# A linear-attention kernel on one Trainium2 core: the last three output stores move from SP's hardware DMA queue to GpSimd's software DMA queue

## The chip, the core and the metric

The kernel runs on one core of one Trainium2 chip. The metric is device time in microseconds (us) of one execution. TensorE (PE), VectorE (DVE), ScalarE (ACT), GpSimd (POOL) and SyncE (SP) each run their own instruction stream; transfers between HBM and the on-chip memory SBUF are issued by SP (a queue that the profile calls hardware_dynamic) or by GpSimd (software_dynamic), and are carried by 16 DMA engines.

## What is computed

Q, K and V have shape (8, 12, 512, 64), float32. For each of the 96 heads:

```
Qf = maximum(0, Q) + 1;  Kf = maximum(0, K) + 1
KV = Kf^T V                      # 64 x 64
out = (Qf KV) / (Qf sum(Kf) + 1e-10)
```

There is no softmax and no 512 x 512 matrix. Each input is read once (12.58 MB each, 37.75 MB in all), and 12.58 MB are written.

## The kernel before

The 96 heads are 48 pairs, four pairs to a group, so there are 12 groups (NG = 12, `last` = 11). Two groups share one step's input tiles and one output tile: `outs[s]` with s = g // 2 holds the results of groups 2s and 2s + 1, and a group's own part of it is every second slot, 4 slots of 512 floats in each of 128 partitions, 1 MiB.

**Loads.** `load` (L105), `load_q` (L119) and `load_rest_q` (L96) are issued on GpSimd, since they also convert float32 to bfloat16; each input's two groups come in one DMA that puts 1 MiB into SBUF (2 MiB out of HBM). Only the first half-step of Q is loaded plain, over SP (L93). Input tiles have two buffers, so a load waits until the buffer's former content has been consumed.

**Compute.** `k_features` and `q_features` (L146, DVE) make the features; `v_blocks` (L157; L164 on DVE, L162 on ACT) puts V into a block layout whose extra columns of ones give the sum of Kf; `keys_values` (L175) multiplies on PE and ACT copies the result; `transposes` (L193) turns the query features; `out_matmuls` (L206) multiplies, and `norms` (L223; L231 reciprocal, L232 multiply, both on DVE) divides and writes the float32 result into `outs`. Each group's `norms` is four pairs of a reciprocal and a multiply.

**Stores.** `store(g)` (L131) writes group g's 1 MiB. The order of everything is written out by hand (L256 on). Stores 0 to 4 are issued in loop turn 7, store 5 in turn 8, store 6 in turn 9, store 7 after that, and stores 8 to 11 at the very end (L313), each on its engine's instruction stream behind whatever that engine was given before. Stores 0 to 9 go over GpSimd (L135). Store 10 goes over SP (L138), and store 11 goes over SP as two halves (L141): the first may leave when head half h = 0 of group 11 has been normalized, the second after h = 1.

**The end of the program.** After the last store SP waits (as L340 in the profile) in turn for the completion of every DMA and of the other engines' work. All five engines then meet at a barrier, GpSimd clears the semaphores, and they meet once more. Each engine drains itself (a DRAIN instruction, also L340) before it signs in at the barrier.

**Semaphores of the software queue.** GpSimd's DMAs use eight completion semaphores in turn. The DMA that reuses a semaphore is held until the DMA eight places before it has landed; for store g that is store g - 8 from g = 8 on, and a load before that.

Of the kernel before, what the change touches and what calls it, by code (L numbers as in the profile page):

```python
# [19 lines left out]
def kernel(  # L20
# [19 lines left out]
    nc = tc.nc  # L40
# [8 lines left out]
    NP = 4  # L49
    NG = NPAIR // NP  # L50
# [36 lines left out]
    outs = {}  # L87
# [43 lines left out]
    def store(g):  # L131
        s = g // 2
        o_to = o_dram[:, 2 * NP * s : 2 * NP * s + 2 * NP]
        if g < NG - 2:
            nc.gpsimd.dma_start(out=o_to[:, g % 2 : 2 * NP : 2], in_=outs[s][:, g % 2 : 2 * NP : 2])  # L135
            return
        if g == NG - 2:
            nc.sync.dma_start(out=o_to[:, 0 : 2 * NP : 2], in_=outs[s][:, 0 : 2 * NP : 2])  # L138
            return
        for h in range(2):  # L140
            nc.sync.dma_start(  # L141
                out=o_to[:, 2 * h + g % 2 : 2 * NP : NP], in_=outs[s][:, 2 * h + g % 2 : 2 * NP : NP]
            )

    def feature(dst, src):
        nc.vector.tensor_scalar(  # L146
# [109 lines left out]
    with tc.manual_schedule():  # L256
# [18 lines left out]
        for g in range(last - 1):  # L275
            if g % 2:
                transposes(g - 1)
            k_features(g)
            v_blocks(g)
            if g >= 2:  # L280
                output(g - 2)
            if g % 2:
                transposes(g)
            else:
                q_features(g)
                q_features(g + 1)
            keys_values(g)
            if g % 2 and g // 2 + 2 < NG // 2:
                load_pair(g // 2 + 2)
            if g == NG - 5:  # L290
                for done in range(g - LAG):
                    store(done)
            if g >= NG - 5:
                store(g - LAG)
# [5 lines left out]
        v_blocks(last)  # L300
        keys_values(last - 1)
        store(last - 1 - LAG)
        q_features(last - 1)
        q_features(last)
# [40 lines left out]
```

## Time and profile before

| | |
|---|---|
| Time, median of 3 runs | 126.48 us (126.4 to 126.58) |
| Time of the profiled execution | 126.1 us |
| Its span, from the first to the last instruction | 124.3 us |
| Mean granted TensorE clock | 0.823 |
| Busy: DVE, PE, ACT, POOL | 89.6, 63.5, 59.6, 25.7 us |
| Packets: software queue, hardware queue | 10592 and 1216 |
| Last multiply of group 11 (L232) starts | 112.85 us |
| Last store issued (L141) | 113.6 us |

The span is what the profile covers; 1.8 us of the profiled execution's own time lie outside it. An instruction that issues a DMA ends when the issue is done; the data land later, and "us to landing" counts from the start of the issue to the last of the 16 DMA engines' completion signals. Two kinds of record in the trace stand behind the page's lines: each packet that a DMA engine moved, with queue, start, duration and size; and each completion signal. DMA busy shares can come out a little above 1, because the records of consecutive packets overlap.

### The profile page before, as it was taken

What the parts mean: (1) busy time and instruction counts of PE and PEld (TensorE: products, weight loads), DVE (VectorE), ACT (ScalarE), POOL (GpSimd) and SP (SyncE); (2) the same over time, 40 slices, a digit from 0 to 9 for tenths busy, and PEclk for the clock granted to TensorE, in tenths of its full rate; (3) what the DMA queues carried; (4) which work ended last, traced back from release to release, by engine and by line L of the source; (5) the groups of instructions that cost most, each with busy time, mean ns of one, the idle gap of its engine ahead of it and who ended that gap; (6) DMA issues with size and microseconds to landing.
All of it is one profiled execution on the core that took longest, in us unless ns stands there. A gap on an engine that the chain in (4) does not pass through costs nothing.

```text
span 124.3 us, 2346 instructions
## 1 busy us (share of the span) xinstructions
PE 63.5 (51%) x960; PEld 52.0 (42%) x960; DVE 89.6 (72%) x190; ACT 59.6 (48%) x86; POOL 25.7 (21%) x53
## 2 busy tenths in 40 slices
PE   0000864500593837629775494928964888652000
PEld 0000754400482737418664383816742757521000
DVE  4885744206999989997999989999169999695000
ACT  7505079606019881866539568393577065300000
POOL 6992021200001400222002392202202200200000
PEclk9999999965579999995899769995596579985555
DMA  3999999999999999999999999999999999999994
GB/s 90 327 211 217 205 208 212 214 214 213 208 211 212 215 223 204 211 213 219 209 212 212 213 215 210 216 208 216 219 287 420 420 419 416 406 415 416 415 409 155
DMA packets 11819, 32.13 MB, mean 258 GB/s; under 512 B 544, under 2 KB 544, under 8 KB 11680
## 3 DMA queue, kind: packets, MB, share of 16 engines
q0 software_dynamic: 10592, 28.84, 97.6%
q1 hardware_dynamic: 1216, 3.15, 6.7%
q8 instruction: 7, 0.11, 0.3%
q14 instruction: 4, 0.03, 0.1%
HBM read 37.75 MB, written 12.58 MB: 405 GB/s over the span
## 4 chain that ended last, share of the span: by engine, by line
DMA 40%; DVE 29%; PE 12%; ACT 7%; issue 2%; POOL 1%; POOLq 0%
DMA v_raw<-in_V_dram 40%; DVE o_sb L232 12%; DVE v_all L164 10%; PE kva_ps L180 8%; ACT qt L204 3%; ACT v_all L162 3%; PE qt_ps L201 3%; DVE recip L231 3%; DVE qf L146 2%; DVE kf L146 1%; PE o_ps L214 1%; DVE qt L204 1%; POOL k_raw L115 1%; ACT kva_all L190 1%; ACT kva_all L191 0%
## 5 line engine op out<-in xcount | busy, mean ns | idle before, releaser
L180 PE MATMUL kva_ps<-v_all,kf 128*64 128x260 bf16 x384 | 30.8, 327 | 15.8 <-DVE v_all L164 14.1
L214 PE MATMUL o_ps<-kva_all,qt 128*64 128x130 bf16 x384 | 20.0, 240 | 31.4 <-DVE recip L231 20.4
L232 DVE TENSOR_TENSOR o_sb<-o_ps,recip 128x512 f32<-128x512 f32 x48 | 33.2, 692 | 1.6
L180 PEld LDWEIGHTS <-kf 128*64 128x64 bf16 x384 | 25.5, 134 | 19.4 <-DVE v_all L164 15.1
L164 DVE COPY v_all<-v_raw 32x2048 bf16<-32x2048 bf16 x36 | 25.5, 710 | 10.6 <-DMA v_raw<-in_V_dram 10.2
L214 PEld LDWEIGHTS <-qt 128*64 128x64 bf16 x384 | 14.0, 118 | 36.5 <-issue 18.3
L162 ACT COPY v_all<-v_raw 32x2048 bf16<-32x2048 bf16 x12 | 22.6, 1893 | 11.2 <-DMA v_raw<-in_V_dram 11.0
L204 ACT COPY qt<-qt_ps 128x1024 bf16<-128x1024 bf16 x23 | 22.2, 1015 | 7.6 <-PE qt_ps L201 7.5
L190 ACT CAST kva_all<-kva_ps 64x256 bf16<-64x256 f32 x24 | 8.9, 372 | 28.2 <-PE kva_ps L180 28.1
L201 PE MATMUL qt_ps<-identity,qf 128*128 128x128 bf16 x192 | 15.3, 240 | 1.8 <-ACT qt L204 1.4
L201 PEld LDWEIGHTS <-qf 128*128 128x128 bf16 x192 | 12.8, 108 | 4.4 <-issue 2.9
L115 POOL DMA_DIRECT2D k_raw<-in_K_dram x7 | 5.4, 773 | 40.0 <-DVE kf L146 39.5
L135 POOL DMA_DIRECT2D out_dram<-o_sb x10 | 7.9, 796 | 26.8 <-DVE o_sb L232 8.8
L231 DVE RECIPROCAL recip<-o_ps 128x8 f32<-128x8 f32 x48 | 9.6, 200 | 5.2 <-PE o_ps L214 5.0
L146 DVE TENSOR_SCALAR kf<-k_raw 128x1024 bf16<-128x1024 bf16 x24 | 10.0, 459 | 4.2 <-PE o_ps L214 3.1
L115 POOL DMA_DIRECT2D v_raw<-in_V_dram x7 | 5.3, 757 | 13.5 <-ACT v_all L162 13.5
L146 DVE TENSOR_SCALAR qf<-q_raw 128x1024 bf16<-128x1024 bf16 x22 | 8.0, 420 | 0.0
L249 DVE MEMSET v_all<- 128x2600 f32 x2 | 4.5, 2225 | 1.1 <-issue 1.1
L191 ACT CAST kva_all<-kva_ps 64x4 bf16<-64x4 f32 x24 | 4.0, 168 | 0.0
L121 POOL DMA_DIRECT2D q_raw<-in_Q_dram x5 | 3.5, 706 | 0.0
L250 ACT COPY v_all<-zero 128x1560 f32<-128x1560 f32 x2 | 2.9, 1488 | 0.0
L271 POOL MEMSET kva_all<- 128x130 bf16 x16 | 2.4, 203 | 0.0
(14 smaller groups left out, 6.6 us busy)
## 6 DMA issues: line engine op xcount, KB each, us to landing
out_dram<-o_sb POOLq DMA_DIRECT2D x10, 1024.0 KB, 24.3
k_raw<-in_K_dram POOLq DMA_DIRECT2D x5, 1024.0 KB, 16.8
v_raw<-in_V_dram POOLq DMA_DIRECT2D x5, 1024.0 KB, 18.3
q_raw<-in_Q_dram POOLq DMA_DIRECT2D x5, 1024.0 KB, 22.5
o_sb<-in_Q_dram SPq DMA_DIRECT2D x1, 1024.0 KB, 4.8
k_raw<-in_K_dram POOLq DMA_DIRECT2D x2, 512.0 KB, 9.5
v_raw<-in_V_dram POOLq DMA_DIRECT2D x2, 512.0 KB, 11.2
out_dram<-o_sb SPq DMA_DIRECT2D x1, 1024.0 KB, 10.7
```

Source lines behind the costliest of these rows:

```text
L115: nc.gpsimd.dma_start(out=bufs[x, s][:, ms], in_=drams[x][:, of])
L135: nc.gpsimd.dma_start(out=o_to[:, g % 2 : 2 * NP : 2], in_=outs[s][:, g % 2 : 2 * NP : 2])
L146: nc.vector.tensor_scalar(out=dst, in0=src, scalar1=1.0, scalar2=1.0, op0=ALU.add, op1=ALU.max)
L162: nc.scalar.copy(out=v_all[ps, g % 2, :, :, b * D : b * D + D], in_=v_raw[ps])
L164: nc.vector.tensor_copy(out=v_all[ps, g % 2, :, :, b * D : b * D + D], in_=v_raw[ps])
L180: nc.tensor.matmul(kva_ps[64 * n : 64 * n + 64], lhsT=kf[:, c, n, :], rhs=v_all[:, g % 2, n, c, :], start=(c == 0), stop=(c == C2 - 1),)
L190: nc.scalar.copy(out=kva[ps, :, n, 0:D], in_=kva_ps[ps, 0 : 4 * D].rearrange("p (b d) -> p b d", b=4))
L201: nc.tensor.transpose(qt_ps[:, c, r], qf[:, r, 2 * half + c, :, :], identity)
L204: copy(out=qts[g // 2][:, lo : lo + 2], in_=qt_ps.rearrange("p c r q -> p c q r"))
L214: nc.tensor.matmul(ops[c // 4][64 * j : 64 * j + 64, c // 2 % 2, (c % 2) * W : (c % 2) * W + W], lhsT=qt[:, c, q : q + 16, :], rhs=kva[:, ...
L231: nc.vector.reciprocal(out=recip, in_=cells[:, :, :, :, D:D1])
L232: nc.vector.tensor_tensor(out=o_sb[:, 2 * h + g % 2 : 2 * NP : NP, 4 * i : 4 * i + 4].rearrange("p n (b c) d -> p b c n d", b=2), in0=cell ...
```

## The change

`store` loses its two special cases. Every group, 10 and 11 too, is stored by one GpSimd DMA of 1 MiB in the form that groups 0 to 9 had before.

```diff
     def store(g):
         s = g // 2
         o_to = o_dram[:, 2 * NP * s : 2 * NP * s + 2 * NP]
-        if g < NG - 2:
-            nc.gpsimd.dma_start(out=o_to[:, g % 2 : 2 * NP : 2], in_=outs[s][:, g % 2 : 2 * NP : 2])
-            return
-        if g == NG - 2:
-            nc.sync.dma_start(out=o_to[:, 0 : 2 * NP : 2], in_=outs[s][:, 0 : 2 * NP : 2])
-            return
-        for h in range(2):
-            nc.sync.dma_start(
-                out=o_to[:, 2 * h + g % 2 : 2 * NP : NP], in_=outs[s][:, 2 * h + g % 2 : 2 * NP : NP]
-            )
+        nc.gpsimd.dma_start(out=o_to[:, g % 2 : 2 * NP : 2], in_=outs[s][:, g % 2 : 2 * NP : 2])
```

In the built program, the streams of PE, DVE and ACT keep their instructions and order. GpSimd's stream has 12 stores instead of 10, the two new ones behind store 9 and ahead of its final DRAIN; store 10 reuses the semaphore of store 2, and store 11 that of store 3. SP's stream loses its three stores and keeps the first load and the final waits. In that list of waits, store 11's completion was the last entry before; now it is the last but one, and the SP load's completion stands behind it.

## Prediction

> **What bounds the kernel now.** I read the page first, for the share of the DMA engines, then the end of the span in windows, then the DMA issues, and last the instructions of line L340, the end of the program.
>
> ```profile
> span 124.3 us, 2346 instructions
> DMA  3999999999999999999999999999999999999994
> q0 software_dynamic: 10592, 28.84, 97.6%
> q1 hardware_dynamic: 1216, 3.15, 6.7%
> ```
>
> The DMA engines are busy nine tenths or more from the second slice to the one before the last. No compute engine is near that (DVE 72%). So the kernel is bound by bytes over the DMA engines, and the order of compute matters only where it leaves them idle. The 40% that the chain of waits gives to V loads says the same.
>
> The windows at the end show each engine's busy time, the clock, the DMA share and GB/s:
>
> ```profile
> 95.00:105.00 10.00, 7.74 (x98) 5.89 (x96) 9.76 (x21) 3.70 (x8) 0.75 (x1) 0.71 1.02 418
> 113.80:120.20 6.40, 0.00 (x0) 0.00 (x0) 0.00 (x0) 0.00 (x0) 0.00 (x0) 0.50 1.03 413
> 120.20:121.60 1.40, 0.00 (x0) 0.00 (x0) 0.00 (x0) 0.00 (x0) 0.00 (x0) 0.50 1.05 408
> 121.60:123.10 1.50, 0.00 (x0) 0.00 (x0) 0.00 (x0) 0.00 (x0) 0.00 (x0) 0.50 0.57 219
> 123.10:124.30 1.20, 0.00 (x0) 0.00 (x0) 0.00 (x0) 0.00 (x0) 0.00 (x0) 0.50 0.00 0
> ```
>
> After 113.8 us only DMA works. From 95 to 105 the software queue stores alone at 418 GB/s; from 113.8 to 120.2 both queues share 413; to 121.6 the hardware queue is alone at 408. The two queues share one capacity. From 123.1 on nothing moves: those 1.2 us are the end of the program.
>
> The issues by line, with the time to landing:
>
> ```profile
> L138 SPq DMA_DIRECT2D out_dram<-o_sb x1: 392/392/392, 110.2 to 110.2; - x1
> DMA to landing us min/median/max: 10.7/10.7/10.7
> L141 SPq DMA_DIRECT2D out_dram<-o_sb x2: 372/372/372, 111.9 to 113.6; - x2
> DMA to landing us min/median/max: 9.9/10.1/10.3
> L135 POOL DMA_DIRECT2D out_dram<-o_sb x10: 754/754/1052, 71.9 to 105.9; - x10
> DMA to landing us min/median/max: 14.8/24.3/28.8
> ```
>
> The last half of store 11 is issued at 113.57 and lands 9.87 us later, at 123.44. Store 9, the last on GpSimd, is issued at 105.86 and lands after 14.75 (the minimum of its row), at 120.61. Ten and fifteen us for 0.5 and 1 MiB are queueing.
>
> Last, line L340:
>
> ```profile
> L340 SPq EVENT_SEMAPHORE  x10: 17/28/28, 116.8 to 124.3; - x10
> L340 POOLq DRAIN  x3: 51/96/16045, 105.8 to 124.1; - x3
> L340 SPq DRAIN  x3: 7/7/7, 123.5 to 123.8; - x3
> L340 ACTq DRAIN  x2: 14/465/916, 106.5 to 123.8; - x2
> L340 DVEq DRAIN  x2: 19/374/730, 112.9 to 123.9; - x2
> ```
>
> Columns are minimum, median and maximum ns, then first and last start. The row to see is POOLq's: one DRAIN of **16.045 us**, which by its length is the first, starting at 105.84, so it ended at 121.89. All that POOL had left then was store 9. The issue instruction took 0.75 us, but the DRAIN stayed until **1.27 us after store 9 had landed** (121.89 - 120.61). The long DRAINs of ACT and DVE last no more than 0.92 us, about one instruction. In this kernel POOL's DRAIN costs nothing: SP's wait for store 11 ends at 123.45, 1.57 us after it. SP's own DRAINs end at 123.58, POOL takes the sign-in at 123.61, and the span ends 0.72 us later, at 124.33.
>
> **The change, part by part.**
>
> *Bytes and rate.* The stores hold the same 12 MiB. By the landing records, stores 0 to 4 on the software queue alone landed at 95.79, 98.31, 100.80, 103.31 and 105.82: 2.51 us each. Store 7 landed at 113.40, just before the hardware queue's first packet (113.79). Four stores more at 2.51 land at 113.40 + 4 x 2.51 = 123.44, where the last one lands today. So sharing two queues neither gains nor costs: **0**. Bounds: packet records say 160 ns for 4096 B on the software queue and 84 ns for 2048 B on the hardware queue, so the moved 2 MiB would take 1024 x 84 / 16 = 5.38 us of each DMA engine against 512 x 160 / 16 = 5.12, a gain of 0.26 us at most, if packets didn't overlap. The landings show that they do; I take them, as whole transfers. The slowest pure stretch, 105.82 to 110.88 for two stores, would cost 4 x 0.02 = 0.08.
>
> *Issue.* SP loses three issues (1.14 us), behind which only its final waits stand: nothing. POOL gains two of 0.75 us. Store 9 shows POOL's reaction: its last multiply ended at about 105.57 and the issue began at 105.86, 0.3 us later, where SP needs 0.03. Store 11 would be issued near 113.8 to 114.6 instead of 111.9 and 113.6. This is covered: at 113.57 the packet records still leave 3.46 MiB, 2.46 without store 11, which is 6.2 us of work. So nothing, and had the queue been empty, about 1 us. The DMAs whose semaphores stores 10 and 11 reuse (stores 2 and 3) landed at 100.80 and 103.31, so those waits don't bite. Nothing else stands behind them on POOL but the DRAIN, and no load is left.
>
> The Trainium skill speaks against this step: in "DMA: Bandwidth & Descriptors", section "Specifications", the software path's first byte comes after about 1 us and the hardware path's after about 0.6. Exposed, that would add an estimated 0.4 us by the page; here SP's store 10 had its first packet 3.6 us after its issue, so both latencies lie under queued work.
>
> *SP's final waits.* One more entry stands behind store 11's completion. Consecutive satisfied entries were 0.06 us apart (120.70, 120.76, 120.82). **+0.07** on SP's side.
>
> *POOL's DRAIN.* This is the part that the diff doesn't show. The last software DMA is now store 11, landing at 123.44. With the trail of before, the DRAIN ends at 123.44 + 1.27 = 124.71, POOL looks at the sign-in about 0.04 later (as at the start of the span), at 124.75, instead of 123.61: **+1.14**. It takes the place of SP's +0.07, which is over by then. The trace shows this trail once, so its size is uncertain. From below: if the DRAIN ends with the landing, SP's +0.07 sets the end. From above: if it looks at the queue now and then and 1.27 was one period, up to 2 x 1.27 = 2.54, that is +2.41. I take 1.27, the one row there is.
>
> By "Perfetto Trace Analysis", section "DMA Instruction — SWDGE (GPSIMD)", the software issue ends for the profile when the last descriptor is written, and the processor completes right after. Taken alone this would leave the DRAIN nothing to wait for, and a sum of +0.07; the 16.045 us of the DRAIN behind a 0.75 us issue speak otherwise.
>
> **Sum.** The profiled execution took 126.1 us, 1.8 outside its span: 126.1 + 1.14 = 127.24. It lies 0.38 under the median of the runs shown, so I put the difference on the median: 126.48 + 1.14 = **127.6 us**, 0.9% slower.
>
> **Rivals.**
>
> *The DRAIN isn't tied to the landing* and its end at 121.89 was chance, or its trail vanishes when the DMA engines are otherwise idle. Then SP's list sets the end: +0.07, 126.55, no change that can be told (0.2%, 0.25 us, is about what a measurement of this kernel can tell). For it: one occurrence only, and nothing else in the span tests it. Against it: 16 us is far over anything POOL executed. Chance 0.18.
>
> *Faster: the software queue's larger packets.* At 160 against 2 x 84 ns the moved stores take up to 0.26 us less, and if POOL's DRAIN doesn't stand in the way the time is 126.48 - 0.26 = 126.2. It decides if the engines run at the packets' own durations and the trail is below 0.1 us. For it: 418 against 408 to 413 GB/s. Against it: the landings, which come out equal. Chance 0.06.
>
> *The DRAIN is tied to the issue, not the landing* (16 us after it). Then it ends at about 114 + 16 = 130, and the time is near 132.5. For it: 16.045 is near a round number. Against it: store 9's landing explains 14.75 of it. Chance 0.04.
>
> **How the numbers follow.** The forecast, a DRAIN that trails the last landing, has 0.72, and by itself 126.9 to 128.6 (a trail of 0.55 to 2.3 us). With the first rival the range is 126.45 to 128.6, which leaves out the last two rivals and a little of the forecast's own tail. Faster: 0.06. Same: the first rival, with the forecast's smallest trails, 0.18. Slower: 0.76.
>
> **What would show it.** The last store lands at 123.3 to 123.6; POOL's long DRAIN ends 1 to 1.5 us after that, and SP's L340 waits are over before it; the stretch without DMA after the last packet grows from 1.2 to some 2.3 us. The software queue alone moves 415 to 420 GB/s until about 122. I am wrong if POOL's DRAIN ends with the last landing, if the last landing itself moves by more than 0.3 us, or if the DMA engines idle anywhere between 105 and 121.

## Result and profile after

The changed kernel takes **127.4 us** (median of 5 executions, 127.25 to 127.67) against 126.48 us before (126.28 to 126.88): 1.0071 times as long, 95% interval 1.0048 to 1.0094. It became slower by 0.9 us; the forecast was 1.1 us (127.6). The page after, in the lines that answer to those of before:

```profile
span 125.6 us, 2345 instructions
DMA  2999999999999999999999999999999999999990
q0 software_dynamic: 11136, 30.94, 100.7%
q1 hardware_dynamic: 144, 1.05, 2.2%
```

The hardware queue keeps only the first load. The DMA engines are as busy as before, but the last of the 40 slices is now empty. The windows at the end (instructions' busy time by engine, granted clock, DMA share, GB/s) show that the transfers didn't get slower:

```profile
113.80:120.20 6.40, 0.00 (x0) 0.00 (x0) 0.00 (x0) 0.00 (x0) 0.00 (x0) 0.50 1.02 417
120.20:121.60 1.40, 0.00 (x0) 0.00 (x0) 0.00 (x0) 0.00 (x0) 0.00 (x0) 0.50 1.00 410
121.60:123.10 1.50, 0.00 (x0) 0.00 (x0) 0.00 (x0) 0.00 (x0) 0.00 (x0) 0.50 0.51 208
123.10:125.60 2.50, 0.00 (x0) 0.00 (x0) 0.00 (x0) 0.00 (x0) 0.00 (x0) 0.50 0.00 0
```

417 GB/s stand where two queues together had 413, and the engines run out of work at the same place, 123.1 us. What grew is the stretch behind it: 2.5 us without a transfer instead of 1.2. The end of the program, now line L331, and the stores, now L134:

```profile
L331 POOLq DRAIN  x3: 51/87/12226, 112.7 to 125.4; - x3
L331 SPq DRAIN  x3: 7/7/7, 123.7 to 125.1; - x3
```

```profile
L134 POOL DMA_DIRECT2D out_dram<-o_sb x12: 752/753/980, 71.4 to 112.7; - x12
DMA to landing us min/median/max: 10.9/23.2/29.6
```

Columns of the DRAIN rows and of L134: minimum, median, maximum ns, then first and last start. Store 11 is issued at 112.68 and lands 10.85 us later, the row's minimum, at 123.53. SP signs in at 123.74, when all its waits are over. GpSimd's DRAIN starts at 112.66 and lasts 12.226 us, so it ends at 124.89, 1.35 us behind the landing. The barrier is entered at 124.93, and the span ends 0.70 us later. SP stands ready for 1.15 us.

### The profile page after: what moved, and what is told of

Same layout as the page of the kernel before. It is cut to its first block, busy times and chain, and to the rows that moved or that the text cites. A ratio compares the mean times of both kernels' runs of the same rounds, so it can differ in the third digit from the quotient of the medians.

```text
span 125.6 us, 2345 instructions
## 1 busy us (share of the span) xinstructions
PE 63.3 (50%) x960; PEld 51.9 (41%) x960; DVE 89.5 (71%) x190; ACT 59.6 (47%) x86; POOL 27.2 (22%) x55
## 4 chain that ended last, share of the span: by engine, by line
DMA 50%; issue 12%; POOL 8%; ACT 7%; DVE 6%; PE 6%; POOLq 1%; DVEq 0%
DMA v_raw<-in_V_dram 29%; DMA out_dram<-o_sb 21%; PE kva_ps L171 4%; DVE v_all L155 3%; ACT qt L195 3%; ACT v_all L153 3%; DVE o_sb L223 2%; POOL kva_all L262 2%; POOL k_raw L115 2%; POOL out_dram L134 2%; POOL v_raw L115 2%; PE o_ps L205 1%; PE qt_ps L192 1%; POOLq L331 1%; ACT kva_all L181 1%
## 5 line engine op out<-in xcount | busy, mean ns | idle before, releaser
L134 POOL DMA_DIRECT2D out_dram<-o_sb x12 | 9.5, 790 | 32.6 <-DVE o_sb L223 10.0
```

## Experiments

A theory was set against rivals. **Theory:** GpSimd's last DRAIN ends about 1.3 us after the last software DMA has landed, and the final barrier waits for it. **Rivals:** the halves of store 11 mattered (A); each MiB over the software queue costs 0.46 us (B); further ones stand in the expectations. Edits of `store` are to the changed kernel. Ratios are to the kernel before, run on the same chip as the edited one, with 95% intervals. Landings and the DRAINs' ends come from the traces' records.

### Both stores back on SP, whole

```diff
+        eng = nc.sync if g >= NG - 2 else nc.gpsimd
-        nc.gpsimd.dma_start(out=o_to[:, g % 2 : 2 * NP : 2], ...)
+        eng.dma_start(out=o_to[:, g % 2 : 2 * NP : 2], ...)
```

> Stores 10 and 11 over SP, each whole; stores 0 to 9 over GpSimd. This undoes the change of queue and keeps store 11 in one DMA. Theory (GpSimd's last DRAIN ends about 1.3 us after the last software DMA has landed, and the final barrier waits for it): store 9 is the last software DMA and lands near 120.6, the DRAIN is over by 122, SP's waits set the end: 126.5, as before, ratio to before 0.999 to 1.001. Rival A (the halves of store 11 were what mattered): stays at 127.4. Rival B (each MiB over the software queue costs 0.46 us of rate or latency): 126.5.

Measured: 126.37 us, ratio 0.9994 (0.9963 to 1.0025). The gain of before is back without the halves, so rival A falls. GpSimd's long DRAIN and SP's:

```profile
L332 POOLq DRAIN  x3: 51/102/16050, 106.0 to 124.2; - x3
L332 SPq DRAIN  x3: 7/7/7, 123.7 to 124.0; - x3
```

The DRAIN ends at 106.03 + 16.05 = 122.08, well ahead of SP's sign-in at 123.7; store 9 landed at 120.81, 1.27 us before its end.

### Stores 8 to 11 on SP

The same edit with `g >= NG - 4`.

> Stores 8 to 11 over SP, whole; stores 0 to 7 over GpSimd. Theory: the DRAIN ends even earlier, about 1.3 us after store 7's landing, and nothing is won by it, because the last landing sets the end: 126.5, ratio 0.998 to 1.002. Rival B (each MiB moved off the software queue saves 0.46 us): 126.48 - 0.92 = 125.6.

Measured: 126.39 us, ratio 1.0025 (0.9994 to 1.0057). Moving two more MiB off the software queue won nothing, against rival B's 0.9 us. One detail of the theory was off: store 7 didn't land early. The software queue now shared the DMA engines longer, and store 7 landed at 119.69; the DRAIN ended at 120.88, 1.19 us later. The last landing, 123.46, was where it was.

### One of the two stores on SP

The same edit with `g == NG - 2` (store 10 on SP, store 11 on GpSimd), and with `g == NG - 1` (the reverse).

> Store 10 over SP, store 11 over GpSimd. Theory: the last software DMA, store 11, lands among the last, at 123.0 to 123.5, so the DRAIN ends at 124.3 to 124.9 and the time is 127.1 to 127.5 although one of the two stores is back on SP. Rival B (cost in proportion to the MiB moved): 126.9 to 127.0, with the DRAIN over before SP's waits. Rival A (halves): 127.4 too, but with the DRAIN over early.

> Store 11 over SP, whole; store 10 over GpSimd. Theory: the time follows store 10's landing on the software queue plus 1.3 us. The two queues share the DMA engines, so that landing lies anywhere between 121.5 and 123.4, and the time between 126.5 and 127.5; in the trace the DRAIN must end 1.2 to 1.5 us after it, and the span about 0.75 us after the later of the DRAIN and SP's last DRAIN. Rival B: 126.9 to 127.0 with the DRAIN over before SP's waits. Rival C (the DRAIN ends a fixed time after GpSimd's last issue, 16.0 us before and 12.2 us after the change): no fixed number fits both already.

Measured: 127.41 us, ratio 1.0084 (1.0051 to 1.0116), with store 10 on SP; 127.43 us, ratio 1.0095 (1.0059 to 1.0131), with store 11 on SP. One store on SP gives nothing of the gain; rival B's half gain isn't there. The second is the more telling, for here SP has the store that is issued last:

```profile
L332 POOLq DRAIN  x3: 51/87/15552, 109.4 to 125.4; - x3
L332 SPq DRAIN  x3: 7/7/7, 123.9 to 125.2; - x3
```

Sharing the DMA engines, store 10 on the software queue landed at 123.60 and store 11 on SP's at 123.75. The DRAIN ended at 109.36 + 15.55 = 124.91, 1.31 us behind store 10, and one us behind SP, which was done at 123.93. What counts is not which store is issued last but when the last software DMA lands.

### ACT in place of SP

The same edit with `nc.scalar if g >= NG - 2`.

> Stores 10 and 11 over ACT's hardware queue, whole; SP issues no store; stores 0 to 9 over GpSimd. Theory (what costs is only that the last DMA is a software one): 126.5 as before, ratio 0.998 to 1.002. Rival E (SP as the issuer is what helps, because it also holds the final waits): 127.4, as after the change.

Measured: 126.34 us, ratio 0.9978 (0.9949 to 1.0007). ACT's hardware queue does as well as SP's; rival E falls. Store 9 landed at 121.55 and the DRAIN ended at 122.82, 1.27 us later.

### The lag alone, on idle DMA engines

A small store behind all others, to the kernel before:

```diff
+        s = last // 2
+        o_to = o_dram[:, 2 * NP * s : 2 * NP * s + 2 * NP]
+        nc.gpsimd.dma_start(out=o_to[:, 2 * NP - 1, C - 1], in_=outs[s][:, 2 * NP - 1, C - 1])
```

and the same with `nc.sync`.

> The kernel before, with one small store added at the very end over GpSimd: 128 x 64 floats (32 KB) of store 11's last slot written a second time with the same values. It waits for store 11 to land, so it runs alone on idle DMA engines. Theory: it is issued near 123.5, lands 1.5 to 2.5 us later, and the DRAIN ends 1.2 to 1.5 us after that landing: 3.5 to 5 us slower than before, 130 to 131.5. Rival F (the lag is one of busy DMA engines or of a large transfer, 64 KB for each engine): the DRAIN ends within 0.3 us of the landing and the time is about 1.2 us less, near 129.

> The same as the run with the small repeated store over GpSimd, but with that store over SP. Theory: issued near 123.5, landed about 2 us later, and no lag behind it: 2 to 2.5 us slower than before, 128.5 to 129; so 1.3 to 2.5 us faster than the same store over GpSimd, 1.3 of it the lag of the DRAIN. Rival F: the two differ by less than 1 us.

Measured: 129.87 us over GpSimd, ratio 1.0235 (1.0149 to 1.0321); 128.23 us over SP, ratio 1.0105 (1.0011 to 1.0200), two executions each. Both cost a little less than expected. The row of the small store's issue and its landing, and the final DRAINs, over GpSimd:

```profile
L317 POOL DMA_DIRECT2D out_dram<-o_sb x1: 551/551/551, 124.0 to 124.0; - x1
DMA to landing us min/median/max: 1.7/1.7/1.7
```

```profile
L343 POOLq DRAIN  x3: 51/96/3173, 124.0 to 127.7; - x3
```

The store is issued at 124.05, lands at 125.79, and the DRAIN ends at 124.03 + 3.17 = 127.20, 1.41 us after it. So a DRAIN that ends over a microsecond behind the landing needs neither busy DMA engines nor a large transfer (32 KB here), and rival F falls. The spans differ by 1.97 us (128.0 and 126.0): the small store lands 0.71 later over GpSimd (125.79 against 125.08), and from the landing to the end it is 2.17 against 0.91.

### When does the DRAIN do its work?

First a GpSimd copy that waits for the last multiply, with stores 6 to 11 on SP.

```diff
+        eng = nc.sync if g >= NG - 6 else nc.gpsimd
...
+        late = const.tile([P, 1], FP32, name="late")
+        nc.gpsimd.tensor_copy(out=late, in_=outs[last // 2][:, 2 * NP - 1, C - 1, D - 1 : D])
```

> Stores 6 to 11 over SP, whole; GpSimd stores only 0 to 5, and ends with a copy of one float per partition that waits for the last multiply of group 11, so that its last DRAIN starts near 113 us, after its own DMAs have landed. Theory (the DRAIN waits until the software DMAs are done, with a lag): the last software DMA, store 5, lands before 112, so the DRAIN is short, under 0.5 us, and the time is as before, 126.3 to 126.7. Rival D (a DRAIN behind any software DMA costs 1.3 us by itself): the DRAIN lasts 1.2 to 1.5 us from its start, with the same time, since SP's waits end later.

This run didn't test what it was meant to: six MiB on SP's queue shared the DMA engines so long that store 5 landed only at 120.30 instead of before 112. The DRAIN ran from 113.61 to 121.41, 1.11 us past that landing. 126.98 us, ratio 1.0028 (0.9999 to 1.0057); its last landing was late, 124.37, and why was not tried.

So the DRAIN was held back until store 11 had landed, by a memset at the very end, to the kernel before and to the changed one:

```diff
+        nc.gpsimd.memset(outs[last // 2][:, 2 * NP - 1, C - 1, D - 1 : D], 0.0)
```

> The kernel before, and at the very end one GpSimd memset of one float in each partition of group 11's output tile. It waits for SP's store 11 to have read that tile, so GpSimd's last DRAIN starts near 123.6 us, about 3 us after store 9, the last software DMA, has landed (120.6). Theory with the lag counted from the landing (GpSimd has long tidied up by then): DRAIN under 0.3 us, time 126.6 to 127.0. Rival D (the DRAIN itself does 1.3 us of work after software DMAs): the DRAIN lasts 1.2 to 1.4 us from its start, time 127.6 to 128.0.

> The changed kernel with the same memset, which here waits for the last software DMA itself (store 11, landing near 123.5), so that the DRAIN starts about 0.2 us after the landing instead of 11 us before it. Theory with the lag counted from the landing: the DRAIN still ends 1.25 to 1.4 us after the landing, the memset hides in it, time as after the change, 127.3 to 127.6. Rival D: the DRAIN takes 1.2 to 1.4 us from its own start, so the end moves with the memset, and the time is 127.6 to 128.0.

Measured: 128.85 us, ratio 1.0171 (1.0121 to 1.0220), and 129.05 us, ratio 1.0195 (1.0150 to 1.0241). Both are above all that was expected. The long DRAIN, first of the kernel before with the memset, then of the changed one:

```profile
L341 POOLq DRAIN  x3: 51/96/2645, 123.6 to 126.8; - x3
```

```profile
L332 POOLq DRAIN  x3: 51/87/2815, 123.8 to 127.0; - x3
```

Store 9 had landed 1.76 us before the first DRAIN began, and yet it took 2.65 us. So the lag isn't time that passes after a landing, as I had taken it: the DRAIN itself has work to do, 2.54 and 2.70 us from the memset's end, twice the lag. If that is so, a DRAIN placed earlier should take the work away from the last one:

```diff
+        nc.gpsimd.drain()
         nc.gpsimd.memset(outs[last // 2][:, 2 * NP - 1, C - 1, D - 1 : D], 0.0)
```

> The kernel before with the late memset, and ahead of that memset an explicit DRAIN on GpSimd, behind its last store. Theory G (a DRAIN has 2.6 us of work of its own when software DMAs have been issued since the DRAIN before it; started early, about half is done while it waits and 1.3 us stay behind the last landing; after that a second DRAIN finds nothing to do): the explicit DRAIN ends 1.2 to 1.4 us after store 9's landing, about 123.2; the memset runs near 123.6 and the final DRAIN lasts under 0.3 us; time 126.7 to 127.0, some 2 us less than the same kernel without the explicit DRAIN (128.85). Rival H (a DRAIN behind a late GpSimd instruction takes 2.6 us whatever was issued): final DRAIN 2.5 to 2.8 us, time 128.8.

> The changed kernel with the late memset and an explicit DRAIN ahead of it. Theory G: the explicit DRAIN ends 1.25 to 1.4 us after store 11's landing, near 124.9, then the memset, then a final DRAIN under 0.3 us: time 127.6 to 127.9, some 1.3 us less than without the explicit DRAIN (129.05) and 0.2 to 0.4 more than the changed kernel itself. Rival H: the final DRAIN takes 2.5 us or more, time about 130.

Measured: 126.53 us, ratio 1.0014 (0.9987 to 1.0041), and 127.75 us, ratio 1.0100 (1.0081 to 1.0118). The added DRAIN saves 2.3 and 1.3 us by the medians against the two kernels without it; these ran on another chip, and by the ratios it is 2.0 and 1.2 us. The explicit DRAIN and the final ones, first of the kernel before, then of the changed one:

```profile
L315 POOLq DRAIN  x1: 19409/19409/19409, 103.7 to 103.7; - x1
```

```profile
L342 POOLq DRAIN  x3: 39/96/182, 123.7 to 124.4; - x3
```

```profile
L306 POOLq DRAIN  x1: 10909/10909/10909, 114.1 to 114.1; - x1
```

```profile
L333 POOLq DRAIN  x3: 39/87/182, 125.1 to 125.8; - x3
```

The explicit DRAINs end at 103.71 + 19.41 = 123.12 and 114.13 + 10.91 = 125.04, 1.27 and 1.35 us behind the last software landing (121.85 and 123.69). After them, behind the same late memset, the final DRAIN takes 0.18 us instead of 2.65 and 2.82. Rival H (a late GpSimd instruction makes it long) falls, theory G stands.

The traces also show what the work grows with. In eleven of them the long DRAIN began over 6 us ahead of the last software landing. Its lag behind that landing follows the number of software DMAs in the program, the 20 loads and the stores on GpSimd:

| Software DMAs | Lag, us | Traces |
|---|---|---|
| 26 | 1.108 | stores 6 to 11 on SP |
| 28 | 1.188 | stores 8 to 11 on SP |
| 30 | 1.271 | five, the kernel before among them |
| 31 | 1.311 | two, one of the last stores on SP |
| 32 | 1.353 and 1.354 | the changed kernel, with and without the explicit DRAIN |

That is a straight line of 0.041 us for each software DMA; drawn on to none it ends at 0.04 us, an extrapolation. The late DRAINs, 2.54 us behind 30 of them and 2.70 behind 32, are twice the lags in the table. The DRAIN at the program's start, ahead of any software DMA, is as short as the final ones behind an explicit DRAIN (0.18 us in all 14 traces; here the changed kernel's):

```profile
L320 POOLq DRAIN  x1: 181/181/181, 0.3 to 0.3; - x1
```

The run with the small store fits too: with 31 software DMAs its DRAIN ended 2.60 us after the issue instruction (124.60 to 127.20), the whole work, so that its 1.41 us behind the landing are not the lag of the other runs. That the number counts and not the bytes is likely, since a store of 32 KB came out near one of 1 MiB, but that is one trace.

## Why the prediction was right, step by step

- **Bytes and rate, 0: right to 0.1 us.** The last landing moved from 123.44 to 123.53. From store 0's landing to the last one it is 27.58 us after (95.96 to 123.53) and 27.65 before (95.79 to 123.44): the software queue alone gained 0.07 us for the stores, within the bound of 0.26. Store 0 landed 0.17 us later in this execution, before anything that the change touches.
- **Issue, 0: right.** GpSimd issued store 11 at 112.68, 0.30 us after its last multiply had ended (112.39), as estimated, under 10.85 us of queueing. DVE ended 1.15 us earlier than in the profile of before, and nothing came of it.
- **SP's list, +0.07: right.** Two entries behind the landing, at 123.55 and 123.61, and SP's sign-in at 123.74, 0.06 us later behind the landing than before; GpSimd hid it, as forecast.
- **The DRAIN, +1.14: right in kind and nearly in size.** Between the two profiled executions GpSimd took the sign-in 1.32 us later (124.93 against 123.61): the forecast's 1.14, 0.10 for the landing and 0.08 for a lag of 1.35 instead of 1.27. The 0.08 is a term that the prediction did not have, the price of two more software DMAs; the lag of the one row that it took was for 30 of them. The medians are 0.92 us apart. The rest is the profiled execution of before, at 126.1 us a quick one (0.38 under its median); the one after was 127.4, at its median. So executions differ by more than the forecast was off, and that the median came within 0.2 us of it is partly luck.
- **The bounds of the lag.** From below, a DRAIN that ends with the landing, is shown wrong by every trace here. From above, a look at the queue now and then with a period of 1.27, doesn't fit either. In the eleven traces of the table the lag was 1.11 to 1.35 us, and equal to 1 ns where the number of software DMAs was; looks with such a period would have spread it from 0 to 1.27 or from 1.27 to 2.54.
- **The rivals.** The DRAIN was tied to the landing, so the first rival falls; it is not tied to the issue (12.2 us after the change, 16.0 before); the larger packets could have given no more than the 0.07 above, and GpSimd's DRAIN stood in the way.

What the prediction did not have: it took the lag for a delay after the landing. The runs show 2.5 to 2.7 us of work in the DRAIN, some 0.08 us for each software DMA issued before it. A DRAIN that begins early leaves half of it, 1.1 to 1.35 us, for after the landing. What is done for each DMA, and why one half of it is left until the last landing, stays open.

## What to carry to other kernels

This program ends when the latest engine signs in at the barrier, so look at the DRAINs there as well as at the last landing. Let the last transfers go over a hardware queue, and enough of them that the last software DMA lands at least 1.3 us before the end (with 30 software DMAs; the lag was 0.04 us shorter for each one fewer): here two stores of 1 MiB sufficed and one gave nothing, because the queues share the DMA engines. In this queue, 10 us deep, it didn't matter for the last landing which engine issued a transfer, 0.3 us sooner or later, or in how many pieces.

## What the hardware showed beyond that

- The software queue moved its stores in packets of 4096 B at 160 ns, the hardware queue in packets of 2048 B at 84 ns; whole transfers took the same, 2.51 us a MiB on either queue alone (on SP's, from store 10's landing at 121.10 to store 11's at 123.60 in the run with both whole on SP). Half a MiB there took 1.264 us (the kernel before).
- With several stores waiting on the software queue, SP's store 10 got its first packet only 3.6 us after its issue (110.21 to 113.79 in the kernel before); its first load, with no other traffic, after 1.0 us.
- On idle DMA engines the small store took 1.46 us from issue to landing over SP and 1.74 over GpSimd, and GpSimd began 0.58 us after the landing that it waited for (123.47 to 124.05), SP 0.02.
